# Paged attention with keys and values in separate tiles, and weight buffers as fixed columns of one tile

## The chip, the cores and the metric

The kernel runs on one core of a Trainium2 chip. The metric is device time in microseconds of one execution, the median of several runs. The core has TensorE (PE, whose weight loads are listed apart as PEld), VectorE (DVE), ScalarE (ACT), GpSimd (POOL) and SyncE (SP), which here mainly issues DMAs; SPq is its instruction queue, worked off in order. Each engine works through its own instructions in order and waits on semaphores for the others.

## What is computed

One inference step of a two-layer decoder, for a prompt of 512 tokens and a sample group of 8 batches with 4 new tokens each. Both groups share the weights and travel together as 544 columns of a transposed activation `x` (1024 features, in 8 tiles of 128 partitions).

- Layer 0: RMSNorm, one input projection, Mamba-2 heads and sliding-window attention, output projection.
- Layer 1: RMSNorm, projections to q, k, v and a forget gate, then *forgetting attention* ("fox"): 16 query heads over 4 key/value heads of 64 features, with a bias from the running sum of the log forget gates. The prompt is swept in 128-query blocks. A sample batch attends to 1024 cached tokens, which lie in 8 pages of 128 tokens each somewhere in a pool of 80 pages (a page table says where), and to its own 4 new tokens.
- Each layer: cross-attention to 256 memory tokens (whose keys and values for the prompt are projected in the kernel), then a SwiGLU feed-forward with 2816 hidden features.

```python
def fox_attend(q, k, v, cum, q_off):
    ...
    bias = cq[..., :, None] - c[..., None, :]
    mask = jnp.arange(tk)[None, :] <= (q_off + jnp.arange(tq))[:, None]
    return gqa_attend(q, k, v, mask=mask, bias=bias)

def swiglu(xn, w_in, w_out):
    g, u = jnp.split(xn @ w_in, 2, axis=-1)
    return (jax.nn.silu(g) * u) @ w_out
```

## The kernel before

**Arithmetic.** Each large product is done as three matmuls of rounded parts: weights and activations are split into a high part (a cast on ACT, L151) and a low part (a subtraction on DVE, L152), and high x high, high x low and low x high are added up in PSUM (`acc3`, L169). `wpiece` (L141) loads one weight piece of 128 x 1024 into a `raw` tile and splits it into `wh` and `wl`. These come from a pool of two, three and three buffers, in which a new tile takes whichever buffer is free.

**Order.** The program is written for a planner (the tile framework's scheduler): it takes the instructions in the order in which the code issues them as a priority, simulates the engines and their waits, and fixes one order for each engine. The planner also places every tile in SBUF, from its first to its last use, and adds a wait where a tile takes bytes that another held. `after(a, b)` adds no semaphore: it only keeps the planner from placing `a` ahead of `b`. Generators such as `linear_steps` give filler matmuls step by step.

**Tiles.** `H` (L119) is a set of 13 equal slots of 8704 bytes a partition. Nearly everything large lives in it: `x`, split activations (`xh`, `xl`, `oh`, `ol`), prompt keys, transposed probabilities (`PT`), memory tiles, and the cached pages.

**Forgetting attention (`odd`, L975).** Half of the query heads (m = 0) runs first: the last four query projections (their operands are `xh`, `xl`) are issued as filler, one step after every fourth head. Then `fill()` (the projection of the memory keys and values of layer 1: tiles `mem`, `memh`, `meml`, `mkv`) becomes the filler, and the second half (m = 1) runs. In between the heads of m = 1 stand the steps of `fox_sample` (L1155), at the places that `FOX_AT` lists. A prompt head (`fox_prompt`, L1075) is a chain: bias and scores on TensorE, maximum on DVE, exponential on ACT, reciprocal on DVE, scaling on POOL, transposes on TensorE, copies on ACT and DVE, product with the values.

`fox_sample` works on *pairs* of batches (G = 0 to 3). For a pair it loads 16 page numbers from a table tile into registers of SP (L1168; the table itself is loaded by a DMA on ACT's queue), and issues 16 page loads of 256 KB (L1172), each of which brings a page's keys and values side by side:

```python
t = [self.H("kv")[:, 0:2048].rearrange("p (g x) -> p g x", g=4) for _ in range(2)]
for g in range(8):
    d = nc.sync.dma_start(t[g // 4][:, g % 4], I["fox_kv"][bass.ds(page[8 * b2 + g], 1)]...)
    self.after(d, gate)
```

So a pair holds four `H` slots, each with keys and values of four pages, from the first load to the last value matmul. `gate` is the DVE addition at L1193 of the pair before, which follows its scores. The four steps of a pair are: scores; softmax; transposes of the probabilities; product with the values and the copy back into `q`.

**Feed-forward (`ffn`, L1484).** The first four of 22 hidden tiles are done directly (`plain`). For the other 18 `factors` (L1451) loads 1 MB of weights into `fr` (two buffers) and forms seven split operands for a product of Strassen's kind, whose activations `operands` (L1417) prepared from `xn` (two buffers). The splits `s3`, `s4` are issued with the others, at the start of a unit. Products of the finished hidden tiles with the output weights are filler: `pair` (L1517) loads two column blocks at once, 512 KB.

Of the kernel before, what the change touches and what calls it, by code (L numbers as in the profile page):

```python
# [9 lines left out]
F32 = mybir.dt.float32  # L10
# [9 lines left out]
P = 128  # L20
# [5 lines left out]
NP = 640  # L26
# [76 lines left out]
class Net:  # L103
    def __init__(self, nc, tc, ctx, I, O):
# [6 lines left out]
        self.wp = pool("weights")  # L111
# [28 lines left out]

    def wpiece(self, src, kt, w):  # L141
        nc = self.nc
        n = kt * w
        raw = self.wp.tile([P, 1024], F32, tag="raw", bufs=2, name=self.nm("raw"))
# [4 lines left out]
        hi = self.wp.tile([P, 1024], F32R, tag="wh", bufs=3, name=self.nm("wh"))  # L149
        lo = self.wp.tile([P, 1024], F32R, tag="wl", bufs=3, name=self.nm("wl"))  # L150
# [177 lines left out]
    def setup(self):  # L328
        nc, I = self.nc, self.I
        self.room = self.pers.tile([P, 4 * NT + NP + 2 * NT], F32, name="room")  # L330
        self.room_at = self.norms = 0
# [643 lines left out]
    def odd(self, st, nxt, fill):  # L975
        nc, tc, I, O = self.nc, self.tc, self.I, self.O
        with ExitStack() as es:
# [53 lines left out]
            with tc.tile_pool(name="fox", bufs=1) as fx:  # L1031
                self.pvs, self.heads = [], 0
                K2 = self.stack_k(kT)
# [17 lines left out]
                smp = self.fox_sample(q, kTs, Qb, ncs, V, lf, fx, S, sel)  # L1051
# [23 lines left out]
    def fox_prompt(self, q, K2, V, ncum, oh16, fx, m, c, at=(), smp=None):  # L1075
# [3 lines left out]
        Q = self.stack_q(fx.tile([P, 1024], F32R, tag="QS", bufs=2, name=self.nm("QS"))[:, 0:1024], q, m, tok)  # L1079
        PT = [self.H("PT")[:, 0:2048].rearrange("p (k r i t) -> p k r i t", k=2, r=2, i=4) for _ in range(c // 2 + 1)]  # L1080
        for r in range(2):
            for i in range(4):
# [10 lines left out]
                pr = fx.tile([P, 512], F32, tag="P", bufs=3, name=self.nm("pr"))  # L1093
# [61 lines left out]
    def fox_sample(self, q, kTs, Qb, ncs, V, lf, fx, S, sel):  # L1155

        nc, I = self.nc, self.I
        c = self.cst
        tp = self.psum("tp", [P, 16])
        self.mm(tp[0:32], self.Ub, lf[0:32, 4], True, True)  # L1160
        nc.vector.tensor_scalar(ncs, tp[0:32].unsqueeze(2).to_broadcast([32, 16, 4]), -1.0, None, ALU.mult)
        gate = d = self.last
        self.sample_q(q, Qb)
        for G in range(4):
            kv = []
            tab = fx.tile([1, 16], I32, tag="tab", bufs=2, name=self.nm("tab"))
            self.after(nc.scalar.dma_start(tab, I["pages"][:, 16 * G:16 * G + 16]), d)
            page = [nc.sync.value_load(tab[0:1, x:x + 1], min_val=0, max_val=79) for x in range(16)]  # L1168
# [315 lines left out]
    def ffn(self, l, st, nxt):  # L1484
        nc, tc, I = self.nc, self.tc, self.I
        with tc.tile_pool(name=f"ffn{l}", bufs=1) as fp:
# [110 lines left out]
            for n in range(FLEAD, NHID):  # L1597
# [4 lines left out]
                if p:  # L1602
                    last(p, 2)
# [153 lines left out]
```

## Time and profile before

| | |
|---|---|
| median of three runs | 1714.89 us (1711.19 to 1715.05) |
| the profiled execution | 1717.13 us |
| its span, first to last instruction | 1715.3 us |
| mean granted TensorE clock | 0.986 |
| busy: PE, PEld | 97%, 89% of the span |
| busy: DVE, ACT, POOL | 68%, 45%, 20% |
| DMA | 189.24 MB, mean 110 GB/s |

The busy share of PE is a bound from above: matmuls are pipelined and each one counts to its modelled end, so a stretch of short matmuls that wait for one another can look nearly full. Weight loads (PEld) show better how dense a stretch is. In a row such as `1060.00:1110.00 50.00, 44.48 (x325) ...` the first numbers are the stretch (us from the start of the span) and its length, then come the busy time and number of instructions of PE, PEld, DVE, ACT and POOL, the granted clock, the busy share of the DMA engines, and GB/s. A row on waits names the engine and line that waited, what ended the wait, and total, number and longest. In a row of one line or tile the durations are minimum, median and maximum in ns, followed by the start of the first and the last.

### The profile page before, as it was taken

To read this page: it belongs to the slowest core of one execution; us is meant where nothing else is said; L and a number is where in the kernel's file an instruction comes from. 1 tells how busy PE (TensorE), PEld (TensorE's weight loads), DVE (VectorE), ACT (ScalarE), POOL (GpSimd) and SP (SyncE) were. 2 spreads that over 40 slices of the span, in tenths; PEclk is the share of its full clock that TensorE was granted. 3 is DMA by queue.
4 is the path that set the end of the run, shared out by engine and by line. 5 is a ranking of instruction groups with operands and counts; after the bars stand their busy time and mean duration, and the time that the engine had idled before them with its cause. 6 is when DMAs were issued, how large, how long until landed. Compare 5 with 4: busy or idle time off the path is not lost.

```text
span 1715.3 us, 32061 instructions
## 1 busy us (share of the span) xinstructions
PE 1667.1 (97%) x12848; PEld 1532.7 (89%) x12848; DVE 1172.5 (68%) x2180; ACT 767.4 (45%) x1567; POOL 340.5 (20%) x508
## 2 busy tenths in 40 slices
PE   6999999998999999999999999899999999999997
PEld 6988889876997999999999997555898999999997
DVE  7667668877766886767767466335577787777663
ACT  5355435444545444444445245325445354444443
POOL 5022323676422300000002013002222300000002
PEclk9999999999999999999999999899999999999999
DMA  5211323137433243232214313453533232323221
GB/s 183 66 50 50 128 85 131 50 126 244 171 99 136 62 148 111 74 111 81 92 53 155 119 62 119 158 172 118 200 127 121 99 111 87 111 78 108 86 76 53
DMA packets 57393, 189.24 MB, mean 110 GB/s; under 512 B 6076, under 2 KB 16092, under 8 KB 49628
## 3 DMA queue, kind: packets, MB, share of 16 engines
q1 hardware_dynamic: 55556, 184.83, 31.8%
q8 instruction: 101, 1.65, 0.4%
q10 hardware_dynamic: 1608, 1.83, 0.4%
q0 software_dynamic: 80, 0.52, 0.1%
q14 instruction: 48, 0.39, 0.1%
HBM read 172.22 MB, written 14.95 MB: 109 GB/s over the span
## 4 chain that ended last, share of the span: by engine, by line
PE 90%; DVE 3%; DMA 3%; POOL 1%; ACT 1%; issue 1%; SPq 0%; DVEq 0%; ACTq 0%; POOLq 0%
PE ps L135 65%; PE ps L1482 22%; PE ps L138 3%; DMA kv<-fox_kv 1%; DMA raw<-we_x 1%; POOL room L412 1%; DVE xl L241 0%; SPq L1172 0%; DVE wl L152 0%; DMA x<-x 0%; DMA mem<-mem 0%; DVE xf L1434 0%; DVE meml L241 0%; POOL sq L408 0%; DVE x L305 0%
## 5 line engine op out<-in xcount | busy, mean ns | idle before, releaser
L135 PE MATMUL ps<-xh,wh 128*128 128x256 f32 (+1 forms) x1152 | 338.8, 295 | 8.8 <-ACT wh L151 7.9
L135 PE MATMUL ps<-xl,wh 128*128 128x256 f32 (+1 forms) x1152 | 338.9, 295 | 1.2 <-DVE xl L241 1.0
L135 PE MATMUL ps<-xh,wl 128*128 128x256 f32 (+1 forms) x1152 | 337.1, 294 | 2.0 <-DVE wl L152 2.0
L1482 PE MATMUL ps<-xf,fh 128*128 128x272 f32 x1728 | 331.1, 288 | 0.0
L1482 PEld LDWEIGHTS ps<-xf,fh 128*128 128x128 f32 x1728 | 271.5, 188 | 1.1 <-ACT ft L1567 0.7
L1482 PE MATMUL ps<-xf,fl 128*128 128x272 f32 x864 | 244.5, 290 | 1.9 <-DVE fl L1466 1.9
L135 PEld LDWEIGHTS ps<-xh,wh 128*128 128x128 f32 x1152 | 219.4, 191 | 12.9 <-ACT wh L151 7.9
L135 PEld LDWEIGHTS ps<-xl,wh 128*128 128x128 f32 x1152 | 219.4, 191 | 7.2 <-issue 4.9
L135 PEld LDWEIGHTS ps<-xh,wl 128*128 128x128 f32 x1152 | 219.3, 191 | 3.2 <-DVE wl L152 2.2
L151 ACT CAST wh<-raw 128x1024 fp32r<-128x1024 f32 (+1 forms) x128 | 130.3, 1020 | 161.1 <-PE ps L135 92.4
L250 POOL TENSOR_TENSOR room<-room,sq 128x256 f32<-128x256 f32 (+1 forms) x96 | 86.8, 907 | 485.8 <-ACT sq L249 483.9
L152 DVE TENSOR_TENSOR wl<-raw,wh 128x1024 fp32r<-128x1024 f32 (+1 forms) x128 | 160.6, 1256 | 28.2 <-PE ps L135 13.6
L1482 PEld LDWEIGHTS ps<-xf,fl 128*128 128x128 f32 x864 | 160.7, 188 | 2.4 <-DVE fl L1466 2.4
L135 PE MATMUL ps<-hl,oh 128*128 128x256 f32 (+1 forms) x512 | 147.2, 288 | 0.0
L135 PE MATMUL ps<-hh,oh 128*128 128x256 f32 (+1 forms) x512 | 146.7, 289 | 0.4 <-ACT oh L1521 0.4
L135 PE MATMUL ps<-hh,ol 128*128 128x256 f32 (+1 forms) x512 | 146.8, 288 | 0.0
L1466 DVE TENSOR_TENSOR fl<-fr,fh 128x1024 fp32r<-128x1024 f32 x108 | 131.5, 1221 | 13.7 <-ACT fh L1465 13.7
L1465 ACT CAST fh<-fr 128x1024 fp32r<-128x1024 f32 x108 | 113.2, 1052 | 33.3 <-DVE fr L1473 18.8
L135 PEld LDWEIGHTS ps<-hh,oh 128*128 128x128 f32 x512 | 96.3, 189 | 0.8 <-ACT oh L1521 0.8
L135 PEld LDWEIGHTS ps<-hl,oh 128*128 128x128 f32 x512 | 96.4, 188 | 0.0
L135 PEld LDWEIGHTS ps<-hh,ol 128*128 128x128 f32 x512 | 96.0, 188 | 0.0
L1534 DVE TENSOR_TENSOR x<-x,ps 128x256 f32<-128x256 f32 (+1 forms) x128 | 55.1, 434 | 43.9 <-PE ps L135 43.3
(427 smaller groups left out, 3733.9 us busy)
## 6 DMA issues: line engine op xcount, KB each, us to landing
fr<-wfi SPq DMA_DIRECT2D x36, 1024.0 KB
or<-wfo SPq DMA_DIRECT2D x32, 512.0 KB
kv<-fox_kv SPq DMA_DIRECT2D x64, 256.0 KB
raw<-wo_e SPq DMA_DIRECT2D x16, 512.0 KB
xk<-mem_k SPq DMA_DIRECT2D x8, 1024.0 KB
xv<-mem_v SPq DMA_DIRECT2D x8, 1024.0 KB
raw<-wfi SPq DMA_DIRECT2D x16, 512.0 KB
raw<-we_x SPq DMA_DIRECT2D x12, 512.0 KB
```

What stands on the lines that cost most here:

```text
L135: self.nc.tensor.matmul(out, lhsT, rhs, start=start, stop=stop)
L138: self.nc.tensor.transpose(out, in_, self.ident[0:k, 0:k])
L151: nc.scalar.copy(hi[:, 0:n], raw[:, 0:n])
L152: nc.vector.tensor_tensor(lo[:, 0:n], raw[:, 0:n], hi[:, 0:n].bitcast(F32), ALU.subtract)
L250: nc.gpsimd.tensor_tensor(acc, acc, sq[:, 0:N], ALU.add)
L412: nc.gpsimd.tensor_tensor(acc, acc, sq, ALU.add)
L1465: nc.scalar.copy(hi, t)
L1466: nc.vector.tensor_tensor(lo, t, hi.bitcast(F32), ALU.subtract)
L1482: self.nc.tensor.matmul(ps, w[a][:, k], x[:, b, k], start=start and k == 0 and i == 0, stop=k == 3 and i == 2, skip_group_check=True)
L1534: nc.vector.tensor_tensor(x, x, ps, ALU.add)
```

## The change

1. The pool of weight buffers is gone. `wraw` hands out two fixed column ranges of `rawt` (part of the tile `room`) in turn, `wsplit` three of `split_t` for high and three for low parts. The feed-forward's `fh` and `fl` come from `wsplit` too, its `f1`, `oh` and `ol` are columns of a tile `fs`, and its output pieces have a raw buffer from `wraw`. A column range is taken strictly in the order of the code.
2. `pair` becomes `four`: one column block of 256 KB for each load, 64 loads in place of 32.
3. `fr` and `xn` share two buffers (`xr`). The splits `s3`, `s4` are issued later in a unit, after the last product of the unit before (`rest`).
4. Prompt queries `QS` (three ranges, two before), probabilities `P` (three) and the sample's work area are columns of `qst` and `prt`.
5. The page pool is two arrays, `fox_k` and `fox_v`. A pair has two key tiles and two value tiles of 8704 bytes, apart from `H`, up to four of each kind. `load(G)` issues the table load (now on SP), 16 register loads, 16 key loads and 16 value loads of 128 KB each.
6. `load(0)` is issued after the sixteenth head of m = 0 (the generator has one more step for it), `load(G + 1)` right after the scores of pair G.

```diff
-        self.wp = pool("weights")
...
+    def wraw(self):
+        self.raws = (self.raws + 1024) % 2048
+        return self.rawt[:, self.raws:self.raws + 1024]
+    def wsplit(self):
+        self.his, self.los = (self.his + 1024) % 3072, (self.los + 1024) % 3072
+        return self.split_t[:, self.his:self.his + 1024], self.split_t[:, 3072 + self.los:3072 + self.los + 1024]
     def wpiece(self, src, kt, w):
-        raw = self.wp.tile([P, 1024], F32, tag="raw", bufs=2, name=self.nm("raw"))
+        raw, hi, lo = self.wraw(), *self.wsplit()
...
-        hi = self.wp.tile([P, 1024], F32R, tag="wh", bufs=3, name=self.nm("wh"))
-        lo = self.wp.tile([P, 1024], F32R, tag="wl", bufs=3, name=self.nm("wl"))
...
-        self.room = self.pers.tile([P, 4 * NT + NP + 2 * NT], F32, name="room")
+        self.room = self.pers.tile([P, 4 * NT + NP + 2 * NT + 2048], F32, name="room")
+        self.split_t = self.pers.tile([P, 6144], F32R, name="split_t")
+        self.rawt = self.keep(2048)
...
+                self.qst, self.prt = fx.tile([P, 3072], F32R, name="qst"), fx.tile([P, 3712], F32, name="prt")
...
+                smp = self.fox_sample(q, kTs, Qb, ncs, V, lf, fx, S, sel)
                 heads = 0
                 for c in range(4):
                     for _ in self.fox_prompt(q, K2, V, ncum, oh16, fx, 0, c):
                         heads += 1
                         if heads % 4 == 0:
                             next(f, None)
+                        if heads == 16:
+                            next(smp)
...
-                smp = self.fox_sample(q, kTs, Qb, ncs, V, lf, fx, S, sel)
...
-        Q = self.stack_q(fx.tile([P, 1024], F32R, tag="QS", bufs=2, name=self.nm("QS"))[:, 0:1024], q, m, tok)
+        self.qs_at = (self.qs_at + 1024) % 3072
+        Q = self.stack_q(self.qst[:, self.qs_at:self.qs_at + 1024], q, m, tok)
...
+        keys, vals = {}, {}
+        gate = self.last
+        def load(G, kd):
+            tab = fx.tile([1, 16], I32, tag="tab", bufs=2, name=self.nm("tab"))
+            self.after(nc.sync.dma_start(tab, I["pages"][:, 16 * G:16 * G + 16]), kd)
+            page = [nc.sync.value_load(tab[0:1, x:x + 1], min_val=0, max_val=79) for x in range(16)]
+            for dst, src in ((keys, "fox_k"), (vals, "fox_v")):
+                for b2 in range(2):
+                    t = fx.tile([P, 4 * NT], F32, tag=src, bufs=4, name=self.nm(src))[:, 0:2048].rearrange("p (g x) -> p g x", g=8)
+                    for g in range(8):
+                        d = nc.sync.dma_start(t[:, g], I[src][bass.ds(page[8 * b2 + g], 1)].rearrange("o p x -> p (o x)"))
+                        self.after(d, gate)
+                        if dst is keys:
+                            kd = d
+                    dst[G, b2] = t
+            return kd
+        kd = load(0, gate)
+        yield
...
-        gate = d = self.last
         self.sample_q(q, Qb)
         for G in range(4):
-            kv = []
-            tab = fx.tile([1, 16], I32, tag="tab", bufs=2, name=self.nm("tab"))
-            self.after(nc.scalar.dma_start(tab, I["pages"][:, 16 * G:16 * G + 16]), d)
-            page = [...]
-            for b2 in range(2):
-                t = [self.H("kv")[:, 0:2048].rearrange("p (g x) -> p g x", g=4) for _ in range(2)]
-                for g in range(8):
-                    d = nc.sync.dma_start(t[g // 4][:, g % 4], I["fox_kv"][...])
-                    self.after(d, gate)
-                kv.append(t)
...
-                        self.mm(sc[u][a:a + 32], lq, kv[b2][u][:, :, 128 * m:128 * m + 128], False, True)
+                        self.mm(sc[u][a:a + 32], lq, keys[G, b2][:, 4 * u:4 * u + 4, 128 * m:128 * m + 128], False, True)
...
-            wk = fx.tile([P, 4 * NT], F32, tag="spr", bufs=1, name=self.nm("spr"))
+            wk = self.prt[:, 1536:3712]
             pr = wk[:, 0:1056]
             gate = nc.vector.tensor_tensor(pr[:, 1024:1056], sn, c[:, C_MN + 32 * G:C_MN + 32 * G + 32], ALU.add)
+            if G < 3:
+                kd = load(G + 1, kd)
             yield
...
-        xn.h = [fp.tile([P, 4 * NT], F32, tag="xn", bufs=2, name=self.nm("xn"))... for _ in range(2)]
+        xn.h = [fp.tile([P, 4 * NT], F32, tag="xr", bufs=2, name=self.nm("xn"))... for _ in range(2)]
...
-        raw = fp.tile([P, 4, 512], F32, tag="fr", bufs=2, name=self.nm("fr"))
+        raw = fp.tile([P, 4 * NT], F32, tag="xr", bufs=2, name=self.nm("fr"))[:, 0:2048].rearrange("p (a w) -> p a w", a=4)
...
-                hi, lo = (fp.tile([P, 2, 512], F32R, tag=g, bufs=3, name=self.nm(g)) for g in ("fh", "fl"))
+                hi, lo = (t.rearrange("p (a w) -> p a w", a=2) for t in self.wsplit())
...
-        split(("s3", "s4"), raw[:, 1:4:2])
-        return out
+        def rest():
+            split(("s3", "s4"), raw[:, 1:4:2])
+        return out, rest
...
-            def pair(src):
-                raw = fp.tile([P, 1024], F32, tag="or", bufs=1, name=self.nm("or"))
+            def four(src):
+                raw = self.wraw()[:, 0:512]
                 self.after(nc.sync.dma_start(raw, src), ready)
-                hi, lo = (fp.tile([P, 1024], F32R, tag=g, bufs=2, name=self.nm(g)) for g in ("oh", "ol"))
+                self.outs_at = (self.outs_at + 1) % 2
+                o = 2048 + 1024 * self.outs_at
+                hi, lo = self.fs[:, o:o + 512], self.fs[:, o + 512:o + 1024]
...
                 second(q)
                 if p:
                     last(p, 2)
+                q["rest"]()
                 third(q, 2)
...
-    A["fox_kv"] = c(np.concatenate([fk, i["cache_fox_v"][0].reshape(80, 128, 256)], 2))
+    A["fox_k"], A["fox_v"] = c(fk), c(i["cache_fox_v"][0].reshape(80, 128, 256))
```

More of the change, by code (lines that the diff above doesn't have):

```diff
@@ L1161, in fox_sample @@
         nc.vector.tensor_scalar(ncs, tp[0:32].unsqueeze(2).to_broadcast([32, 16, 4]), -1.0, None, ALU.mult)
-        gate = d = self.last
         self.sample_q(q, Qb)
         for G in range(4):
-            kv = []
-            tab = fx.tile([1, 16], I32, tag="tab", bufs=2, name=self.nm("tab"))
-            self.after(nc.scalar.dma_start(tab, I["pages"][:, 16 * G:16 * G + 16]), d)
-            page = [nc.sync.value_load(tab[0:1, x:x + 1], min_val=0, max_val=79) for x in range(16)]
-            for b2 in range(2):
-                t = [self.H("kv")[:, 0:2048].rearrange("p (g x) -> p g x", g=4) for _ in range(2)]
-                for g in range(8):
-                    d = nc.sync.dma_start(t[g // 4][:, g % 4], I["fox_kv"][bass.ds(page[8 * b2 + g], 1)].rearrange("o p x -> p (o x)"))
-                    self.after(d, gate)
-                kv.append(t)
             sc = [self.psum("sc", [P, 4, 128]), self.psum("sc", [P, 4, 128])]
@@ L1421, in operands @@
         xn = Big(self, "xn")
-        xn.h = [fp.tile([P, 4 * NT], F32, tag="xn", bufs=2, name=self.nm("xn")).rearrange("p (k t) -> p k t", k=4) for _ in range(2)]
+        xn.h = [fp.tile([P, 4 * NT], F32, tag="xr", bufs=2, name=self.nm("xn")).rearrange("p (k t) -> p k t", k=4) for _ in range(2)]
         for k in range(KD):
@@ L1460, in split @@
             if n == 1:
-                one = fp.tile([P, 2, 512], F32R, tag="f1", bufs=2, name=self.nm("f1"))
+                self.ones_at ^= 1
+                one = self.fs[:, 1024 * self.ones_at:1024 * self.ones_at + 1024].rearrange("p (a w) -> p a w", a=2)
                 hi, lo = one[:, 0:1], one[:, 1:2]
             else:
-                hi, lo = (fp.tile([P, 2, 512], F32R, tag=g, bufs=3, name=self.nm(g)) for g in ("fh", "fl"))
+                hi, lo = (t.rearrange("p (a w) -> p a w", a=2) for t in self.wsplit())
             nc.scalar.copy(hi, t)
@@ L1487, in ffn @@
             t = fp.tile([P, 4 * NT], F32, name="ft")
+            self.fs = fp.tile([P, 4096], F32R, name="fs")
+            self.ones_at = self.outs_at = 0
             U, G = ([t[:, NT * i:NT * i + NT] for i in r] for r in ((0, 1), (2, 3)))
@@ L1554, in begin @@
                 nc.scalar.copy(U[n % 2][:, 0:HT], R)
-                return {"n": n, "w": w, "R": R, "u": U[n % 2], "g": G[n % 2]}
+                return {"n": n, "w": w, "rest": rest, "R": R, "u": U[n % 2], "g": G[n % 2]}
             def second(p):
@@ L1707, in layout @@
     for g, (a, n) in enumerate(FGROUPS):
-        A[f"wfo{g}"] = np.stack([pieces(i["w_ffn_out"][l, 128 * a:128 * (a + n)], n, 256 if n == 4 else 128) for l in range(2)])
+        A[f"wfo{g}"] = np.stack([pieces(i["w_ffn_out"][l, 128 * a:128 * (a + n)], n, 128) for l in range(2)])
     A["conv_state"] = c(i["state_conv"][0].reshape(8, 3, 12, P).transpose(3, 2, 0, 1))
```

14 lines of the change are left out of this document (8 added, 6 removed).

## The prediction

> **What bounds the kernel now.** I read the page's head, then its chain, then the kernel in stretches, then the waits of TensorE and of the DMA-issuing queue (SPq) in the one stretch that stands out.
>
> ```profile
> span 1715.3 us, 32061 instructions
> PE 1667.1 (97%) x12848; PEld 1532.7 (89%) x12848; DVE 1172.5 (68%) x2180; ACT 767.4 (45%) x1567; POOL 340.5 (20%) x508
> PE 90%; DVE 3%; DMA 3%; POOL 1%; ACT 1%; issue 1%; SPq 0%; DVEq 0%; ACTq 0%; POOLq 0%
> 650.00:700.00 50.00, 50.00 (x400) 50.00 (x399) 34.19 (x50) 20.66 (x34) 0.00 (x0) 1.00 0.26 85
> 1005.00:1045.00 40.00, 40.00 (x294) 34.82 (x292) 23.93 (x68) 19.21 (x57) 9.84 (x22) 1.00 0.16 54
> 1060.00:1110.00 50.00, 44.48 (x325) 30.74 (x322) 26.20 (x72) 22.39 (x59) 6.76 (x13) 0.86 0.52 170
> 1110.00:1160.00 50.00, 44.52 (x279) 26.41 (x278) 19.12 (x55) 13.90 (x45) 5.34 (x11) 0.97 0.55 191
> 1160.00:1210.00 50.00, 46.48 (x387) 29.38 (x387) 25.33 (x74) 25.62 (x71) 9.07 (x15) 1.00 0.30 100
> 1091.00:1105.00 14.00, 11.79 (x103) 7.84 (x100) 3.24 (x15) 5.56 (x18) 1.49 (x4) 0.54 0.14 41
> PE ps L135 <- DMA kv<-fox_kv: 7.3, 5, 2.4
> SPq L1172 <- PE ps L135: 28.8, 7, 7.8
> SPq L1168 <- DMA tab<-pages: 13.5, 1, 13.5
> ```
>
> A stretch's columns are its length, busy time of PE, weight loads (PEld), DVE, ACT, POOL, then granted clock, DMA share, GB/s. The feed-forward (650 to 700) is TensorE from end to end: 50.00 of 50. What can move is the odd layer's attention. From 1005 to 1045, prompt heads of its first half run with the query projection as filler, and weights load 34.82 of 40 us, 87%. From 1060 to 1210 the second half of the heads and the sample group's paged attention run, and weight loads are 30.74 + 26.41 + 29.38 = 86.5 of 150 us, 58%. PE looks 90% busy there only because small dependent matmuls are long. TensorE's own waits for K/V are 7.3 us, but SPq waited 28.8 us to place those loads (for buffers that matmuls held) and 13.5 us for the first page table.
>
> When each of the four pairs of batches is scored (kv,odd) and its values are used (kv,spr):
>
> ```profile
> L135 PE MATMUL ps<-kv,odd x16: 592/617/1062, 1073.2 to 1091.3; 128*32 128x512 f32 x16
> L135 PE MATMUL ps<-kv,spr x64: 421/421/423, 1098.0 to 1103.3; 128*32 128x128 f32 x64
> L135 PE MATMUL ps<-kv,odd x16: 589/592/617, 1108.6 to 1122.6; 128*32 128x512 f32 x16
> L135 PE MATMUL ps<-kv,spr x64: 272/273/423, 1138.5 to 1142.5; 128*32 128x128 f32 x64
> L135 PE MATMUL ps<-kv,spr x64: 272/273/297, 1164.0 to 1167.2; 128*32 128x128 f32 x64
> L135 PE MATMUL ps<-kv,odd x16: 589/592/617, 1167.8 to 1181.7; 128*32 128x512 f32 x16
> L135 PE MATMUL ps<-kv,spr x64: 272/273/297, 1188.8 to 1192.6; 128*32 128x128 f32 x64
> L1110 DVE COPY q<-ps x6: 692/692/692, 1059.7 to 1209.8; 128x512 f32<-128x512 f32 x6
> ```
>
> From one pair's last value matmul to the next pair's takes 39.2, 24.7 and 25.4 us, together 89.3; the last head ends at 1209.8, 17 us after the last pair. Loads of the second pair begin at 1102.1 (below), as the first pair's values are being used: with keys and values in one tile, no slot returns before.
>
> **The change, part by part.**
>
> *First load moved forward.* SPq:
>
> ```profile
> L1168 SPq TENSOR_LOAD <-tab x16: 262/262/483, 1047.8 to 1057.0; - x16
> 1060.37 9.95 SPq L1172 DMA_DIRECT2D kv<-fox_kv  x12
> 1083.64 2.27 SPq L1172 DMA_DIRECT2D kv<-fox_kv  x4
> 1085.58 4.71 DMA kv<-fox_kv
> 1102.09 9.84 SPq L1172 DMA_DIRECT2D kv<-fox_kv  x16
> 1131.06 3.96 SPq L1172 DMA_DIRECT2D kv<-fox_kv  x8
> L135 PE MATMUL ps<-xh,wl x74: 274/293/380, 999.8 to 1046.7; 128*128 128x288 f32 x40, 128*128 128x256 f32 x34
> ```
>
> Page numbers are read from 1047.8 to 1057, after SPq's 13.5 us wait; the twelve first page loads follow at 1060, and four more only at 1083.6, for want of the fourth slot. The last of those takes 4.71 us to land, and the first pair's scores end at 1091.3. In the new code the table and page numbers are asked for after sixteen heads of the first half, so that reading them lies in the queue's idle time before 1047. The keys need two slots; the projection's four input tiles are last read at 1046.7 and give them. Sixteen key loads at 0.5 us (eight took 3.96) end at 1055, land by 1060, and are scored by about 1065 between heads. That is 26 us ahead of 1091.3. Bounds: 0 if the slots go to the memory tiles first, 40 if keys find room before 1047. I take 26, since three kv slots were free by the middle 1060s even so.
>
> *Keys freed after scores, values later; half-size loads.* The queue now issues 32 loads per pair, not 16, and the page-table load moves from ACT's queue to it. Page numbers cost 9.2 us a pair (the row of 16), loads 32 x 0.5 = 16, the table's landing about 2 (it blocks the queue): 27 to 28 us a pair of pure queue work, where the old one needed 9.2 + 8 to 10. What queues behind it are the weight loads of the memory projection and of the output projection; both had slack there. Three cycles of 28 are 84 against 89.3: 5 us won, no more, since SPq now paces what buffers paced. Bounds: by the fastest old cycle, 24.7, it would be 15 won; a queue at 0.62 per load (16 in 9.84) would lose 6. Keys come first, so scores need not wait for the values.
>
> Behind a row stands a rule: the Trainium skill, DMA: Bandwidth & Descriptors, Rules for kernel authors, wants small transfers coalesced and each DMA at 1 MiB or more, which speaks against halving them to 128 KB. The row of sixteen 256 KB loads in 9.84 us shows that a queue of them overlaps its fixed part, so the trace does not bear out a full price for each. That page's fixed 2 us for each of the 64 added loads would make the sum 128 us worse, an estimate.
>
> *What is late next.* The heads themselves: max, exponential, reciprocal, scaling, transposes. With the loads out of the way this stretch can at best be as dense as 1005 to 1045: 86.5 / 0.87 = 99 us, which is 51 less than 150. The half clock of 1091 to 1105 (0.54 granted, so at most 14 x 0.46 = 6 us) should go too; that is part of the bound.
>
> The Trainium skill, TensorE: Matmul & The Clock Gate, Why this matters for your kernels, has TensorE at half rate after idle gaps of about 3 us. The longest single wait for kv here is 2.4 us and the clock fell all the same, so the row is harsher than the rule; by the rule alone those 6 us would not be there to win.
>
> *Fixed columns for raw, high and low weights* (two, three and three, as before), prompt queries in three columns (two before), P in three: the same depth, taken in program order. No instruction is added. I take 0, covered by TensorE's queue of matmuls; without that cover a late piece costs its cast and subtraction, 2.3 us (rows below). Bounds -3 to +5 over the even layer, whose buffers are placed anew.
>
> *Feed-forward.*
>
> ```profile
> L1465 ACT CAST fh<-fr x108: 1037/1052/1057, 608.1 to 1655.7; 128x1024 fp32r<-128x1024 f32 x108
> L1465 ACT CAST f<-fr x36: 608/612/619, 609.0 to 1647.6; 128x512 fp32r<-128x512 f32 x36
> L1466 DVE TENSOR_TENSOR fl<-fr,fh x108: 1207/1221/1227, 609.4 to 1656.7; 128x1024 fp32r<-128x1024 f32 x108
> L1466 DVE TENSOR_TENSOR f<-fr,f x36: 682/693/696, 610.5 to 1648.3; 128x512 fp32r<-128x512 f32 x36
> L1521 ACT CAST oh<-or x32: 1032/1041/1057, 616.4 to 1610.8; 128x1024 fp32r<-128x1024 f32 x32
> L1455 SPq DMA_DIRECT2D fr<-wfi x36: 327/328/423, 601.5 to 1625.5; - x36
> L1434 DVE TENSOR_TENSOR xf<-xn,xf x12: 1275/1282/1898, 583.6 to 1378.6; 128x1088 fp32r<-128x1088 f32 x12
> 610.00:620.00 10.00, 8.86 (x64) 8.22 (x64) 9.98 (x13) 7.22 (x10) 1.18 (x1) 1.00 0.19 52
> ```
>
> The 32 output pieces become 64 of half size: ACT 64 x 0.612 - 32 x 1.041 = 6 us more, DVE 64 x 0.693 - 32 x 1.221 = 5 us more, over two feed-forwards in which ACT is busy 20.66 and DVE 34.19 of 50: hidden. The late split of s3 and s4 waits for the previous unit's last product; its use is a third of a unit later, so hidden, at 2.3 us a unit if it weren't (36 units, 83 us: the price of this cover). At the start, raw factors share two slots with the normalized input, so the second raw load can go only when the last operands are split, where the old one went at about 602. DVE idles four of ten us just after that, so these splits can come forward; the start already loses 1.1 us of ten to DVE. I take +2 per feed-forward, bounds -1 and +6: +4 together.
>
> **Sum.** -26 - 5 + 4 = -27. The profiled execution took 1717.13 us (1.8 outside its span), the median of three runs is 1714.89, 2.2 lower. 1714.9 - 27 = 1688.
>
> **Rivals.**
> 1. *The heads close up as well* (p 0.2): with data always there the stretch nears the density of 1005 to 1045. For: no engine is above 26.2 of 50 there. Against: without the memory projection's matmuls as filler after 1130, heads wait for one another. -51 + 4 = -47: 1668.
> 2. *Hidden anyway* (p 0.1): pairs are paced by the heads they are interleaved with, and only TensorE's 7.3 us for kv go, less the feed-forward's 4. 1712.
> 3. *SPq becomes the wait* (p 0.16), slower: in one queue, value loads stand ahead of the next pair's table and page numbers, and they wait for slots that the pair before holds until its value matmuls. Then a cycle is serial: 11 table and numbers, 8 keys, 4.7 landing, 14 scores (1108.6 to 1122.6), 8 values: 46 us, 3 x 46 - 89 = 49 lost against 26 won and 4 for the feed-forward: 1742. It decides from 38 us a cycle ((89.3 + 26) / 3). For: every wait in this queue blocks all behind it. Against: keys return their slots early.
>
> The first skill rule is this rival's: more, smaller transfers.
>
> **How the numbers follow.** The forecast (-15 to -38) has 0.54, rivals 0.2, 0.1, 0.16. A measurement can tell about 0.3%, 5 us. Faster: 0.54 + 0.2 = 0.74; same 0.1; slower 0.16. The range reaches down to the density bound with nothing lost in the feed-forward, 51 less (1664) and 2 for noise, and up to rival 2 with the feed-forward's upper bound, 12 instead of 4: 1720. Outside is left rival 3. The likeliest's own range is 1677 to 1700.
>
> **What would show it.** First pair's scores end near 1065 and the last pair's values near 1160, not 1192.6; the waits of TensorE for keys and values below 3 us; clock 1.00 from 1060 on; the feed-forwards as long as before within 6 us each. It is wrong if page-number reads and loads of one pair take SPq over 38 us, if the scores still end after 1085, or if a feed-forward unit shows a wait that repeats.

## The result, and the profile after

| | before | after |
|---|---|---|
| median (11 runs each) | 1713.68 us (1708.09 to 1715.63) | 1703.70 us (1697.89 to 1706.96) |
| ratio, 95% interval | | 0.9943 [0.9928, 0.9958] |
| profiled execution, its span | 1717.13, 1715.3 us | 1705.22, 1703.5 us |
| mean granted TensorE clock | 0.986 | 0.992 |

Faster by 10 us, 0.57%. The forecast was 1688, 27 us faster. Direction and range held; the size was off by more than half.

The span of the changed kernel, then stretches of it. The columns are those of before: length, PE, PEld, DVE, ACT, POOL, granted clock, DMA share, GB/s.

```profile
span 1703.5 us, 32512 instructions
1010.00:1050.00 40.00, 40.00 (x299) 35.81 (x299) 26.04 (x72) 21.24 (x60) 8.56 (x19) 1.00 0.33 98
1060.00:1110.00 50.00, 47.74 (x370) 31.49 (x368) 30.23 (x84) 24.69 (x72) 9.61 (x19) 1.00 0.44 137
1110.00:1160.00 50.00, 48.85 (x393) 29.76 (x390) 22.71 (x76) 20.70 (x64) 8.73 (x17) 1.00 0.54 159
1160.00:1193.50 33.50, 32.61 (x258) 23.62 (x256) 20.10 (x49) 18.65 (x49) 4.91 (x7) 1.00 0.59 196
```

The work of 1060 to 1210 now ends at about 1194, with the clock at 1.00 throughout; weight loads fill 84.9 of 133.5 us (64%, 58% before). The density of 1005 to 1045 (87%) is far away. Now the sample group: scores of the four pairs, their values, the last prompt heads, and the first and last Strassen unit of the feed-forwards (the copy of its first product).

```profile
L134 PE MATMUL ps<-fox_k,odd x16: 589/592/617, 1074.7 to 1078.3; 128*32 128x512 f32 x16
L134 PE MATMUL ps<-fox_k,odd x16: 592/604/617, 1102.9 to 1109.8; 128*32 128x512 f32 x16
L134 PE MATMUL ps<-fox_k,odd x16: 592/592/617, 1121.2 to 1129.6; 128*32 128x512 f32 x16
L134 PE MATMUL ps<-fox_k,odd x16: 592/604/617, 1147.2 to 1157.9; 128*32 128x512 f32 x16
L134 PE MATMUL ps<-fox_v,prt x64: 272/273/297, 1099.8 to 1101.9; 128*32 128x128 f32 x64
L134 PE MATMUL ps<-fox_v,prt x64: 272/273/297, 1127.4 to 1129.1; 128*32 128x128 f32 x64
L134 PE MATMUL ps<-fox_v,prt x64: 272/273/297, 1149.1 to 1151.5; 128*32 128x128 f32 x64
L134 PE MATMUL ps<-fox_v,prt x64: 272/273/297, 1170.6 to 1173.2; 128*32 128x128 f32 x64
L1125 DVE COPY q<-ps x6: 691/692/692, 1065.4 to 1193.5; 128x512 f32<-128x512 f32 x6
L1554 ACT COPY ft<-ps x36: 373/387/388, 615.2 to 1654.8; 128x272 f32<-128x272 f32 x36
L1589 ACT COPY ft<-ps x36: 369/385/393, 620.6 to 1643.0; 128x272 f32<-128x272 f32 x36
```

(L1554 is the kernel before.) Read against the rows of before:

| stage | before | after | change |
|---|---|---|---|
| start to first unit of feed-forward 0 | 615.2 | 620.6 | +5.4 |
| from there to the first pair's last value matmul | 488.1 | 481.3 | -6.8 |
| to the last pair's (three cycles) | 89.3 | 71.3 | -18.0 |
| to the last prompt head | 17.2 | 20.3 | +3.1 |
| to the last unit of feed-forward 1 | 445.0 | 449.5 | +4.5 |

The sum is -11.8, the difference of the spans (the stretch behind the last unit takes 60.5 us in both). In absolute time the first pair's values came only 1.4 us earlier (1101.9 for 1103.3), although its scores ended 13 us earlier.

Where the lead of the first keys went is seen on SP's queue and in the memory projection (times and lengths of groups of DMA issues, then the matmuls with the memory's high and low parts, and the subtraction that makes the low part):

```profile
1033.49 15.10 SPq L1186 DMA_DIRECT2D fox_k<-fox_k  x16
1078.88 6.56 SPq L1186 DMA_DIRECT2D fox_k<-fox_k  x12
1138.07 16.28 SPq L1186 DMA_DIRECT2D fox_k<-fox_k  x16
SPq L1186 <- PE ps L134: 13.1, 3, 6.9
L134 PE MATMUL ps<-memh,split_t x64: 278/283/384, 1069.5 to 1107.0; 128*128 128x256 f32 x64
L134 PE MATMUL ps<-meml,split_t x32: 279/283/386, 1079.3 to 1106.9; 128*128 128x256 f32 x32
L248 DVE SCALAR_TENSOR_TENSOR meml<-mem,room,memh x8: 476/477/485, 1078.7 to 1081.5; 128x256 fp32r<-128x256 f32 x8
L135 PE MATMUL ps<-meml,wh x32: 278/283/384, 1064.9 to 1107.4; 128*128 128x256 f32 x32
```

The keys are issued from 1033 to 1049, as predicted, but no score matmul starts before 1074.7. In the placed program the memory's low part lies in the bytes of the first key tile, so its subtraction starts at 1078.7, just behind the scores (the trace has it waiting for TensorE), and the filler's low part, which ran from 1064.9 before (last row), runs from 1079.3. The second pair's first key load stood 6.9 us for the first pair's scores too, and left at 1078.88; the third pair's stood 4.9 us for TensorE. Four key tiles at once had no room at these two places; the fourth pair's first key load did not wait for a tile.

### The profile page after: what moved, and what is told of

Its sections match the earlier page's. It is cut to its first block, busy times and chain, and to the rows that moved or that the text cites. A ratio compares the mean times of both kernels' runs of the same rounds, so it can differ in the third digit from the quotient of the medians.

```text
span 1703.5 us, 32512 instructions
## 1 busy us (share of the span) xinstructions
PE 1657.2 (97%) x12848; PEld 1529.4 (90%) x12848; DVE 1179.1 (69%) x2212; ACT 772.8 (45%) x1599; POOL 328.2 (19%) x508
## 4 chain that ended last, share of the span: by engine, by line
PE 89%; DVE 4%; POOL 2%; DMA 2%; issue 1%; ACT 1%; DVEq 0%; ACTq 0%; POOLq 0%
PE ps L134 64%; PE ps L1512 22%; PE ps L137 3%; POOL room L421 1%; ACT split_t L158 0%; DMA lg<-fox_logf,pg 0%; DVE xs L875 0%; DVE split_t L159 0%; POOL sq L417 0%; DVE split_t L1493 0%; DMA room<-wo_e 0%; DVE xn L1450 0%; DVE meml L248 0%; DMA room<-wfi 0%; DMA o_s_ssm<-hb 0%
## 5 line engine op out<-in xcount | busy, mean ns | idle before, releaser
L134 PE MATMUL ps<-xh,split_t 128*128 128x288 f32 (+1 forms) x2304 | 466.1, 294 | 16.6 <-ACT split_t L158 12.0
L134 PEld LDWEIGHTS ps<-xh,split_t 128*128 128x128 f32 x2304 | 372.0, 191 | 23.8 <-ACT split_t L158 13.2
L1512 PE MATMUL ps<-xf,split_t 128*128 128x272 f32 x2592 | 348.9, 289 | 3.1 <-DVE split_t L1493 2.2
L134 PE MATMUL ps<-xl,split_t 128*128 128x256 f32 (+1 forms) x1152 | 338.7, 295 | 1.2 <-DVE xl L248 1.0
L1512 PEld LDWEIGHTS ps<-xf,split_t 128*128 128x128 f32 x2592 | 335.0, 188 | 4.5 <-DVE split_t L1493 3.1
L134 PEld LDWEIGHTS ps<-xl,split_t 128*128 128x128 f32 x1152 | 219.2, 190 | 6.6 <-issue 4.1
L134 PE MATMUL ps<-hh,fs 128*128 128x256 f32 (+1 forms) x1024 | 206.3, 288 | 0.0
L159 DVE TENSOR_TENSOR split_t<-room,split_t 128x1024 fp32r<-128x1024 f32 (+1 forms) x128 | 155.7, 1219 | 30.6 <-ACT split_t L158 29.9
L134 PEld LDWEIGHTS ps<-hh,fs 128*128 128x128 f32 x1024 | 164.9, 188 | 0.4 <-ACT fs L1556 0.4
L134 PE MATMUL ps<-hl,fs 128*128 128x256 f32 (+1 forms) x512 | 147.3, 288 | 0.0
```

What stands on the lines that cost most here:

```text
L134: self.nc.tensor.matmul(out, lhsT, rhs, start=start, stop=stop)
L159: nc.vector.tensor_tensor(lo[:, 0:n], raw[:, 0:n], hi[:, 0:n].bitcast(F32), ALU.subtract)
L1512: self.nc.tensor.matmul(ps, w[a][:, k], x[:, b, k], start=start and k == 0 and i == 0, stop=k == 3 and i == 2, skip_group_check=True)
```

## The experiments

Medians of the runs, and ratios to the kernel before on the same chip (1712.0 to 1714.1 us). The experiments ran on several chips, so kernels of different rows are best compared by their ratios.

| kernel | median us | ratio, 95% interval |
|---|---|---|
| the changed kernel | 1703.70 | 0.9943 [0.9928, 0.9958] |
| old_loads | 1724.47 | 1.0066 [1.0046, 1.0086] |
| late_first | 1714.30 | 1.0000 [0.9987, 1.0014] |
| late_joint | 1711.50 | 0.9982 [0.9967, 0.9998] |
| late_joint_behind | 1711.36 | 0.9983 [0.9970, 0.9997] |
| late_joint_wide | 1718.44 | 1.0036 [1.0019, 1.0053] |
| vals_first | 1722.96 | 1.0056 [1.0036, 1.0076] |
| vals_after_mem | 1700.47 | 0.9926 [0.9906, 0.9947] |
| scores_first | 1706.41 | 0.9957 [0.9941, 0.9973] |
| light_numbers | 1707.07 | 0.9961 [0.9947, 0.9976] |
| gate_first | 1699.21 | 0.9916 [0.9893, 0.9938] |
| gate_first_light | 1697.65 | 0.9912 [0.9890, 0.9933] |
| combined | 1696.59 | 0.9907 [0.9888, 0.9926] |

My first theory (A) after seeing the traces was that the early load was worth nothing and the cycles were worth everything, because keys come free early. The rival (B) was the prediction's own: the early load is the large term.

**old_loads: the columns and the feed-forward by themselves.**

```diff
-            if G < 3:
-                kd = load(G + 1, kd)
...
+                t = [self.H("kv")[:, 0:2048].rearrange("p (g x) -> p g x", g=4) for _ in range(2)]
+                for g in range(8):
+                    d = nc.sync.dma_start(t[g // 4][:, g % 4], I["fox_kv"][bass.ds(page[8 * b2 + g], 1)]...)
```

> The changed kernel with the page loads of the kernel before (keys and values together in four slots a pair, 256 KB each, table on ACT's queue, first load at its old place): what is left is the fixed columns and the feed-forward. The traces have the first Strassen unit of the two feed-forwards 5.4 and 2.6 us later, all of it before that unit. If these come from the feed-forward's own start, this kernel is 6 to 9 us slower than the kernel before (1.0035 to 1.0055), and its forgetting attention takes as long as before. If the columns also matter among the heads, it differs from that by more than 3 us either way.

Measured: +10.3 us on the kernel before, interval 8 to 15; a little more than the 6 to 9 us expected. So this part costs more than twice the 4 us that I had given it. The other half by itself, the new loads with the old weight pool, wasn't tried.

**late_first: the first load at its old place.**

```diff
-                        if heads == 16:
-                            next(smp)
...
                 next(f)
+                next(smp)
```

> The changed kernel, but the first pair's table, page numbers and loads are issued where they used to be (after the first half of the heads and the first step of the memory projection). Theory A: bringing the first load forward gained next to nothing, because the first pair's values were used at 1101.9 instead of 1103.3 us; all of the gain is in the three cycles from pair to pair, which became 18 us shorter. Then this kernel is within 5 us of the changed one: 0.992 to 0.997 of the kernel before (1700 to 1708 us). Since the first key tile then no longer lies in the bytes that the low part of the memory tokens needs, it may even win a few us. Theory B, that of the prediction: the early load is the larger term; without it 10 to 26 us are lost again, 1.000 to 1.010 of the kernel before.

Theory A falls: without the early load the whole gain of the change is gone (1714.3 for 1703.7). Theory B has the amount at the low end of its span, 10.6 us, and not its mechanism: the first pair's values come no later, but all that follows does. Rows of this kernel, as above, with a wait of SP's queue between the two groups of value loads (the profiled execution is this kernel's slowest, 1719.20 us, so its last rows lie some us later than the median's):

```profile
1066.41 2.40 SPq L1185 DMA_DIRECT2D fox_v<-fox_v  x5
SPq L154 <- DVE split_t L159: 10.6, 1, 10.6
1079.97 5.50 SPq L1185 DMA_DIRECT2D fox_v<-fox_v  x11
1088.89 16.63 SPq L1185 DMA_DIRECT2D fox_k<-fox_k  x16
1151.54 17.10 SPq L1185 DMA_DIRECT2D fox_k<-fox_k  x16
L134 PE MATMUL ps<-fox_k,odd x16: 592/604/617, 1158.4 to 1172.9; 128*32 128x512 f32 x16
L134 PE MATMUL ps<-fox_v,prt x64: 272/273/297, 1096.8 to 1098.9; 128*32 128x128 f32 x64
L134 PE MATMUL ps<-fox_v,prt x64: 272/273/297, 1180.1 to 1183.4; 128*32 128x128 f32 x64
```

First values end at 1098.9, 3 us sooner than in the changed kernel. But the value loads stand from 1068.8 to 1080.0: ahead of them in the queue is a weight load of the memory projection, which waits 10.6 us for the subtraction that frees its raw column (L159). The second pair's keys go out at 1088.9 instead of 1078.9, the last pair's end at 1168.6 instead of 1154.4, and its scores end 4.3 us behind them (3.5 in the changed kernel). So the keys of the later pairs leave 6 to 14 us earlier in the changed kernel, and the last pair's values end 10.2 us earlier there. That this lead is what the early load pays is argued from these times and not shown: TensorE itself waited for cached pages only 0.6 us in the changed kernel and 0.2 us in late_first, and light_numbers below has a lead in its last keys without a gain.

**late_joint and late_joint_behind: keys no longer free early; loads issued behind the values.** Pairs 1 to 3 get four tiles that hold keys and values together; in the second kernel `load(G)` moves back to the head of pair G.

```diff
+            both = [[fx.tile([P, 4 * NT], F32, tag="fox_kv", bufs=4, ...)... for _ in range(2)] for _ in range(2)] if G else None
...
+                        out = both[b2][g // 4][:, g % 4, o:o + 256] if G else t[:, g]
```

> As the kernel with the late first load, and in addition pairs 1 to 3 get four tiles that hold keys and values together, so that none comes free before the pair's values are used; number and size of the loads stay. Theory A: the cycles go back to about 30 us each, 12 to 18 us slower than the kernel with the late first load: 1.000 to 1.008 of the kernel before. Theory B: the lifetimes of keys matter little, at most 5 us slower than the kernel with the late first load.

> As the kernel with the late first load and joint tiles for pairs 1 to 3, but the loads of a pair are issued where they used to be in the code: ahead of its scores, behind the values of the pair before, instead of right behind the scores of the pair before. Theory P: the 10 to 13 us between the old page loads and this layout come from the place of issue, a pair ahead; they are lost again: 1719 to 1724 us, 1.003 to 1.006 of the kernel before. Theory T: they come from tiles of their own outside the 13 slots; then it stays within 3 us of 1711.5 (0.9965 to 1.000).

Theory A falls a second time: with the early release of keys undone the kernel is not slower than late_first (0.9982 against 1.0000; if anything 3 us faster). And with joint tiles the place in the code does not matter: 1711.36 against 1711.50 (with separate tiles, or with the early first load, neither edit was tried). Theory T is what is left of the two, but is not shown: tiles of their own, the order within a pair and the size of the loads are still together here.

**late_joint_wide and vals_first: size against order.** Both start from late_joint. The first brings pairs 1 to 3 in sixteen loads of 256 KB; the second keeps the 128 KB loads and issues the values first.

```diff
+                        kd = nc.sync.dma_start(both[b2][g // 4][:, g % 4], I["fox_kv"][bass.ds(page[8 * b2 + g], 1)]...)
```

```diff
-            for dst, src, o in ((keys, "fox_k", 0), (vals, "fox_v", 256)):
+            for dst, src, o in ((vals, "fox_v", 256), (keys, "fox_k", 0)) if G else ((keys, "fox_k", 0), (vals, "fox_v", 256)):
```

> As the kernel with the late first load and joint tiles, but pairs 1 to 3 are loaded in sixteen loads of 256 KB instead of thirty-two of 128 KB. Theory S: SP's queue paces the pairs by now (it works 85 of the 105 us from 1060 to 1165); sixteen loads fewer at 0.52 us are 8 us of queue a pair, the last pair's values come 8 to 16 us earlier, and the time is 1700 to 1706 us (0.992 to 0.995). Theory H: the heads pace, the queue has slack: within 2 us of 1711.5.

> The kernel with the late first load and joint tiles for pairs 1 to 3, sixteen value loads ahead of the sixteen key loads in these pairs (all of 128 KB, as many as before). Theory K: what the halved loads brought is that a pair's keys come ahead of its values, so that scores start on half the bytes; turned round, keys are complete some 8 us later in each pair and the kernel is 5 to 12 us slower than 1711.4 (1.000 to 1.006 of the kernel before), like the one with 256 KB loads (1718.4). Theory N: the order within a pair does not matter, the pair's slots or the heads do: within 3 us of 1711.4 (0.9965 to 1.000).

Theory S misses: sixteen loads fewer a pair cost 7 us. Theory K holds for the 128 KB loads: with the values ahead 11.5 us are lost (12.7 us by the ratios), about what separates old_loads from late_first (10.2 us). Below stand the last pair's loads, its scores and TensorE's wait for keys in vals_first, then keys and scores of that pair in late_joint, then the third pair's scores in old_loads, and the third and the last pair's scores in late_joint_wide:

```profile
1164.27 9.23 SPq L1188 DMA_DIRECT2D fox_kv<-fox_v  x16
1173.68 9.18 SPq L1188 DMA_DIRECT2D fox_kv<-fox_k  x16
L134 PE MATMUL ps<-fox_kv,odd x16: 589/592/617, 1179.9 to 1185.5; 128*32 128x512 f32 x16
PE ps L134 <- DMA fox_kv<-fox_k: 7.5, 6, 2.3
```

```profile
1155.53 14.31 SPq L1188 DMA_DIRECT2D fox_kv<-fox_k  x16
L134 PE MATMUL ps<-fox_kv,odd x16: 589/592/617, 1160.5 to 1172.2; 128*32 128x512 f32 x16
```

```profile
L134 PE MATMUL ps<-kv,odd x16: 589/605/952, 1127.9 to 1151.0; 128*32 128x512 f32 x16
```

```profile
L134 PE MATMUL ps<-fox_kv,odd x16: 592/592/617, 1136.4 to 1144.9; 128*32 128x512 f32 x16
L134 PE MATMUL ps<-fox_kv,odd x16: 592/604/617, 1166.6 to 1178.1; 128*32 128x512 f32 x16
```

Scores end 2.6 us behind the last key load in vals_first (1182.9 to 1185.5) and 2.4 us in late_joint (1169.8 to 1172.2), and TensorE's waits for keys grow from 0.5 us in late_joint to 7.5 us. In old_loads, with keys and values side by side in one load, the third pair's scores are drawn out over 23 us (1127.9 to 1151.0), and all that time they hold both `sc` buffers of PSUM (the memory in which TensorE adds up), which two of three heads need too; in the changed kernel the same pair takes 8.4 us (1121.2 to 1129.6). Side by side alone does not do this: in late_joint_wide that pair takes 8.5 us.

The Trainium skill, DMA: Bandwidth & Descriptors, Rules for kernel authors, wants small transfers made into large ones. Here the larger loads lose (1718.44 for 1711.50). That this is because one transfer then brings what is needed now and what is needed some 25 us later is likely after vals_first, but not shown: in late_joint_wide the last pair's loads, values included, have all left at 1168.1, its scores end at 1178.1, 10.0 us behind (2.4 in late_joint), and TensorE waits only 0.2 us for pages. What held those scores stays open. Tiles of their own (theory T) may be worth some 5 us: old_loads and late_joint_wide both load 256 KB side by side and have ratios of 1.0066 and 1.0036. But these intervals overlap, and the first pair differs too.

**vals_after_mem and scores_first: why the first pair did not come earlier.** The first keeps the first value loads behind the split of the memory tokens, so that the memory's parts get slots of their own; the second issues the first scores ahead of the memory projection.

```diff
-                        self.after(d, gate)
+                        self.after(d, self.memlast if G == 0 and dst is vals else gate)
```

```diff
+                next(smp)
                 f = fill()
...
-FOX_AT = (0, 2, 2, 3), ...
+FOX_AT = (2, 2, 3), ...
```

> The changed kernel with one edge more in the order: the first pair's value loads are kept behind the split of the memory tokens, so that the memory tokens get a slot of their own instead of waiting for the first key tile (in the changed kernel their low part lies in that tile's bytes, and the memory projection, the filler, starts at 1079 us instead of 1064). Theory F: the filler was missing between 1060 and 1079 us and is worth its gap: 5 to 10 us faster than the changed kernel, 0.988 to 0.991 of the kernel before. Theory C: the heads wait for one another there and filler only moves: within 2 us of the changed kernel, 0.993 to 0.9955.

> The changed kernel with the first pair's scores issued right after the query projection, ahead of the memory projection's first step and of the second half of the heads. Theory W: its keys are in place by about 1051 us and the scores came at 1074.7 to 1078.3 only for their place in TensorE's order; now they end by about 1066, as predicted for the change, and the last head ends 5 to 13 us earlier: 0.987 to 0.991 of the kernel before. Theory C: the pairs behind are paced by SP's queue or by the heads, and the end does not move: within 3 us of the changed kernel, 0.992 to 0.996.

```profile
L134 PE MATMUL ps<-meml,split_t x32: 278/283/388, 1066.6 to 1097.7; 128*128 128x256 f32 x32
L134 PE MATMUL ps<-fox_v,prt x64: 272/273/297, 1094.0 to 1095.6; 128*32 128x128 f32 x64
```

```profile
L134 PE MATMUL ps<-fox_k,odd x16: 589/592/617, 1072.0 to 1074.3; 128*32 128x512 f32 x16
L134 PE MATMUL ps<-fox_v,prt x64: 272/273/297, 1100.2 to 1101.9; 128*32 128x128 f32 x64
```

In vals_after_mem (first fence) the filler's low part starts at 1066.6 and the first values end at 1095.6, 6.3 us earlier (4.1 us counted from the first unit of the first feed-forward, which this execution reached 2.2 us sooner). Its median is 3.2 us lower than the changed kernel's, but the intervals overlap (0.9906 to 0.9947, 0.9928 to 0.9958): between the two theories, and not settled. In scores_first (second fence) the scores start 2.7 us earlier, nowhere near 1066, the values end where they did, and the time is no better: theory W falls in so far as the place in the code was not what held them. What scores at 1066 would be worth was therefore not measured. Why the planner keeps the scores at 1072 with the keys in place, and heads of the second half ahead of them, stays open.

**light_numbers: SP's queue relieved.**

```diff
-            page = [nc.sync.value_load(tab[0:1, x:x + 1], min_val=0, max_val=79) for x in range(16)]
+            page = [nc.s_assert_within(nc.sync.value_load(tab[0:1, x:x + 1]), 0, 79, skip_runtime_bounds_check_because="...") for x in range(16)]
```

> The changed kernel, but each page number is read without the check of its bounds: one register load of 0.27 us instead of three instructions that take 0.56 us with their gaps. Theory S: SP's queue paces pairs 2 and 3 of the changed kernel (their keys go out one number and one load in turn from 1111.9 to 1125.6 and from 1138.1 to 1154.4 us, and their scores end 4.0 and 3.5 us behind the last of them). Some 4 us of queue a pair less: the last pair's scores 4 to 9 us earlier, 1694 to 1700 us, 0.988 to 0.992 of the kernel before. Theory H: the heads and the order that the planner fixed pace them; within 2 us of the changed kernel: 0.993 to 0.9955.

```profile
1133.17 9.88 SPq L1186 DMA_DIRECT2D fox_k<-fox_k  x12
1146.97 0.33 SPq L1186 DMA_DIRECT2D fox_k<-fox_k  x1
L134 PE MATMUL ps<-fox_k,odd x16: 592/601/617, 1153.1 to 1159.9; 128*32 128x512 f32 x16
```

The last keys are out at 1147.3, 7 us earlier than in the changed kernel, and the scores end at 1159.9, 2 us later: 12.6 us behind the keys instead of 3.5. The kernel is no faster (1707.07; 3.4 us above the changed kernel, more than theory H allowed, with intervals that overlap). Theory S falls: SP's queue is not what paces the changed kernel. The time that it saved it stood: it waited 25.8 us for TensorE to give tiles back (13.1 in the changed kernel), 19.2 of them for the second pair's first key tile. What holds the last scores is not shown by one run; the heads and the planner's order are what is left.

**gate_first, gate_first_light, combined: the start of the feed-forward.** TensorE's waits for weights (PEld) between 564 and 625 us in the changed kernel:

```profile
PEld ps L134 <- ACT split_t L158: 2.9, 3, 1.4
PEld ps L134 <- DVE split_t L159: 1.0, 1, 1.0
```

In the kernel before no wait for such a piece stands there. Each of the first hidden tiles uses its gate's piece first and its other piece last, but requested them in the other order. Of three columns taken in turn, the next is then the one that the tile frees last; a pool gave out the one that was free. gate_first is vals_after_mem with the two requests exchanged:

```diff
-                wu, wg = (self.wpiece(I["wfi0"][l, 2 * n + r], KD, 128) for r in range(2))
+                wg, wu = (self.wpiece(I["wfi0"][l, 2 * n + r], KD, 128) for r in (1, 0))
```

> The kernel with the first pair's values behind the memory split, and one line more: in the first hidden tiles of the feed-forward the gate's weight piece is requested ahead of the other one. Theory R (columns in turn): three pieces are alive, a tile's two and the first of the next; the column that comes next in turn belongs to the piece whose last matmul ends the tile, although the gate's piece is done 24 matmuls earlier and TensorE stood 1.36, 0.92 and 1.16 us before such pieces in the first feed-forward. With the order turned the column that comes next is the one that is free first; from the last addition of cross-attention to the first Strassen unit it takes about 51 us instead of 54.6 (50.3 in the kernel before), 4 to 6 us in all with the second feed-forward: 0.988 to 0.991 of the kernel before. Rival: the pieces are late for ScalarE's or the DMA's sake; then the 54.6 us stay and the time stays at 0.9926.

The last addition of cross-attention and, above, the first unit, in the kernel before, in the changed one and in gate_first, with gate_first's only wait and its clock right there:

```profile
L305 DVE TENSOR_TENSOR x<-x,ps x16: 405/430/455, 542.6 to 564.9; 128x256 f32<-128x256 f32 x8, 128x288 f32<-128x288 f32 x8
L312 DVE TENSOR_TENSOR x<-x,ps x16: 407/429/455, 543.7 to 565.9; 128x256 f32<-128x256 f32 x8, 128x288 f32<-128x288 f32 x8
L312 DVE TENSOR_TENSOR x<-x,ps x16: 404/428/453, 543.9 to 566.1; 128x256 f32<-128x256 f32 x8, 128x288 f32<-128x288 f32 x8
L1595 ACT COPY ft<-ps x36: 375/385/393, 616.5 to 1637.9; 128x272 f32<-128x272 f32 x36
PEld ps L134 <- DVE fs L1563: 2.1, 1, 2.1
616.00:624.00 8.00, 6.09 (x36) 5.84 (x36) 8.00 (x12) 5.22 (x8) 0.00 (x0) 0.79 0.54 185
```

50.3 us before, 54.7 after, 50.4 in gate_first: theory R holds for this stretch, to the tenth, and misses its 4 to 6 us in all. A wait of 2.1 us for an output piece's subtraction takes its place at 620 us, VectorE being busy 8.00 of 8 there, and the clock falls behind it. By a later product of the same unit (first copy at L1613, 633.1 us) the gain is gone: 67.0 us behind that addition, 67.1 in vals_after_mem. The total moves 1.3 us, within the intervals. The stall moved on to VectorE, which had no slack there before either (9.98 of 10 from 610 to 620 in the prediction's row).

gate_first_light adds the edit of light_numbers to it:

> The kernel with the gate's piece first, and the page numbers read without the check of their bounds. Theory S: a further 4 to 9 us, 1690 to 1695 us, 0.986 to 0.989 of the kernel before. Theory H: within 2 us of that kernel's 1699.2, 0.990 to 0.993.

Light numbers bring 1.6 us here, inside the noise: theory S falls again. combined gives, on top of that, the raw factors and the raw output pieces tiles of their own:

```diff
-        raw = fp.tile([P, 4 * NT], F32, tag="xr", bufs=2, name=self.nm("fr"))[:, ...
+        raw = fp.tile([P, 4 * NT], F32, tag="fr", bufs=2, name=self.nm("fr"))[:, ...
...
-                raw = self.wraw()[:, 0:512]
+                raw = fp.tile([P, 512], F32, tag="or", bufs=2, name=self.nm("or"))
```

> The kernel before this one, and in the feed-forward raw factors and the raw output pieces in tiles of their own, no longer shared with the normalized input and with the turn of the other weight pieces. The wait of 2.07 us that took the place of the removed ones, ahead of an output piece at 620.1 and 1364.6 us, should go if it comes from that sharing (SP waited 11.2 us at the first factor load, output pieces behind it): 2 to 5 us less than the kernel with the light numbers and the gate first. If it comes from the columns of the split factors, nothing changes.

```profile
PEld ps L134 <- DVE fs L1563: 2.2, 1, 2.2
```

The wait stays at 2.2 us, so it isn't the sharing. combined has the lowest median of the study, 1696.59 us, 0.9907 [0.9888, 0.9926], just clear of the changed kernel's interval. Its four edits are clear of the noise only together, and how much each brings isn't shown.

## Why the prediction was right and wrong

- **First load forward, -26: mis-sized, 10.6 us by late_first, and by another path.** The step that failed is "scored by about 1065 between heads". The keys were there (issued by 1049), but the scores came at 1074.7. I had given the two key tiles the bytes that the projection's inputs free; I named the bound that the memory's parts might take them ("0 if the slots go to the memory tiles first") and left out the reverse, in which the filler waits (1079.3 for 1064.9). What held the scores with the keys in place stays open (scores_first). And I counted the first scores' lead in full towards the end, while the first values moved only 1.4 us. The 10.6 us that are there go with a lead of the loads of the later pairs; why they pay is argued, not shown.
- **Cycles, -5: mis-sized and wrongly explained.** From old_loads to late_first the new loads bring 10.2 us without the early one; the three cycles took 71.3 us (89.3 before, 84 forecast). I had put them down to keys freed early and had SP's queue pace the rest. Beside a late first load, early freeing brings nothing (late_joint), and SP does not pace (light_numbers). What pays is that keys come ahead of values, 11.5 us by vals_first. I had that in half a sentence, without a price.
- **Columns and feed-forward, +4: mis-sized, 10.3 us by old_loads.** The steady units take the same time, as predicted (275.9 and 275.5 us from the first to the eighteenth). The loss at the first start is 4.4 us (50.3 to 54.7); around the second it is 4.5 us, counted from the last head to the last unit, with cross-attention in between. The 0 for columns of "the same depth" was the step that failed: in turn is not the same as whichever is free, once pieces are freed in another order than they were requested. Closing that gap brought only 1.3 us in gate_first, as VectorE's lack of slack took its place. The rest of the 10.3 us wasn't traced to its place.
- The sum by runs: -10.6 - 10.2 + 10.3 = -10.5, against -10.0 measured. The three are steps from one run to the next, so that they add up says nothing of their causes. That the direction held is in part luck: the loss was 6 us larger than forecast and the first gain 15 us smaller, and only the cycles, for another reason than the one given, made up 5.
- **Rival 3** (SP's queue becomes the wait, 46 us a cycle) did not come: keys did return early enough, the cycles were 27.2, 22.4 and 21.7 us. **Rival 1** (the heads close up too) did not come either: 64% density, not 87%. **Rival 2** (1712) had the first pair right, "paced by the heads they are interleaved with", and the later ones wrong.
- What I had said would show it: clock 1.00 from 1060 on, right; TensorE's waits for keys and values below 3 us, right (0.6); feed-forwards within 6 us each, right; last values near 1160, wrong (1173.2); scores near 1065, wrong.

## What to carry to other kernels

Before a transfer is moved forward, ask whose bytes it will sit in meanwhile: a tile that arrives 25 us before its use can take the slot of the work that was to cover the time. Where a transfer brings something needed now and something needed later, split it so that the first part arrives first: with loads of the same size and number, the order alone made 11.5 us here. A ring in program order equals a pool of the same depth only if pieces are released in the order in which they were requested, so request first what is released first.

## What the runs showed of the hardware

Most of what separates runs of one kernel goes with the granted clock, and so may much of what separates the two kernels. The changed kernel's eleven runs go from 1697.89 us at a mean clock of 0.996 to 1706.96 us at 0.991; 23 runs of the kernel before, beside the experiments, from 1709.27 at 0.990 to 1720.21 at 0.985. A thousandth of the clock over 1705 us is 1.7 us, and the two series follow it at about 2 us a thousandth (9.1 and 10.9 us over five). By the prediction's rows the kernel before lost at most 8.5 us of clock from 1060 to 1160 (50 x 0.14 + 50 x 0.03), the changed one nothing:

```profile
1090.00:1104.00 14.00, 11.36 (x96) 7.10 (x97) 3.24 (x15) 4.85 (x17) 1.49 (x4) 0.51 0.11 34
```

```profile
1078.00:1092.00 14.00, 14.00 (x103) 9.80 (x96) 7.69 (x19) 3.07 (x6) 0.00 (x0) 1.00 0.49 143
```

The first row is the kernel before, where TensorE was loading weights half the time; the second a comparable stretch of the changed kernel. So a part of the gain may be not time saved by a shorter path, but a clock that no longer falls; how much of it can't be told apart by these runs, since the idle time and the clock go together. The clock fell behind a single wait of 2.1 us too (gate_first, 0.79 from 616 to 624). The Trainium skill, TensorE: Matmul & The Clock Gate, Why this matters for your kernels, gives gaps of about 3 us as the limit; the wait measured here was shorter.
